# Attention inside an encoder layer: ScalarE's and GpSimd's side jobs dealt out one piece to a step

## The chip, the cores and the metric

The kernel runs on one core of a Trainium2 chip. Time is device time in microseconds (us) of one execution, from the profiler or from the runtime. The engines are TensorE (PE, its weight loads are shown as PEld), VectorE (DVE), ScalarE (ACT), GpSimd (POOL) and SyncE (SP, which only issues DMAs here). Each engine takes its instructions strictly one after the other, in an order fixed when the program is built; an instruction may carry waits for other engines or for DMAs, and everything behind it on its engine waits too.

## The reference

One encoder layer over 2048 tokens of width 1024, batch 1, float32:

```
h = rmsnorm(x, g1) * (1 + sc1) + sh1                   # shift, scale, gate from c
q, k, v of 8 stick-breaking heads and 8 chunk heads = h @ w_in      # head width 64
stick-breaking: z = q k^T / 8;  w = sigmoid(z) * prod of sigmoid(-z) over the later keys (strictly causal)
chunk heads:    rms-normed q, k;  softmax over own chunk of 64 + 8 earlier chunks, with a relative bias
x = x + gt1 * (concat(heads) @ w_o)
h = rmsnorm(x, g2) * (1 + sc2) + sh2
x = x + gt2 * (relu(h @ w1)^2 @ w2)
```

## The kernel before

Every float32 operand of a matmul is held as a high part and a remainder, both in a reduced float32 format, and each product is three matmuls. The program has four stretches: projections (to about 405 us), attention (405 to 1290 us), and then the rest of the output projection and the two large products of the MLP, to the end at 2572 us. The change touches attention alone.

Attention runs over units. A stick-breaking unit (`SB`, instructions `z`, `p`, `b`) is one head, a block g of 512 queries and a block c of 512 keys; a softmax unit (`CA`, instructions `cz`, `ct`, `s`, `e`) is one head and a block of 512 queries. Tokens are stored reversed, so a block's own keys come first: for g the units are c = g (the diagonal, where the four query rows of 128 see 512, 384, 256 and 128 keys), then c = g+1 to 3. The list is: for each head SB(2,2), SB(2,3), SB(3,3); all CA with g = 1 to 3; SB with g = 1 and g = 0; CA with g = 0. So the work turns three times from one kind to the other.

Each unit has four steps, one per 128 queries, and the main loop (from line 1298) issues one step after the other. In a step of a stick-breaking unit: TensorE turns a finished weight tile of eight steps earlier (`wt`, four transposes), ScalarE makes the sigmoid of the scores in place (`z`), VectorE scans it into running products (`p`), GpSimd subtracts neighbours (`b`, after a copy of one column into `p`), ScalarE and VectorE split the turned tile (`wth`, `wtl`), TensorE multiplies an older split tile into the accumulator (`acc`) and makes the scores of the next step (`z`). Scores and turned tiles take turns in one ring of four PSUM buffers (`z` of the pool `pz`), so a matmul into it needs VectorE to be done with the tile four back. In a softmax step VectorE adds bias and takes the maximum (`s`), ScalarE makes the exponential (`e`), and GpSimd scales it a step later. Between these TensorE works off pieces of other projections (`fill`, tiles `pf` and `po`), whose results ScalarE copies out (`stf`, `svf`).

When a unit is the last of its head and block, `finish` (line 788) runs a step later: ScalarE copies the two halves of the accumulator to `otmp` and `o`. After the second head of a pair, `total` has GpSimd add them (`o<-o,otmp`, 512 columns) in the next step, and `keep`, two steps later, has ScalarE make the high part (`os<-o`), GpSimd the remainder (`os<-o,os`), and SP store it. These jobs wait in the list `soon`: what a step puts there is issued in the next step, all of it, after that step's own work. At a turn they are put off three steps. `os` has one buffer, in pool `op`. In two blocks the output projection's rows are squared for the next norm (`square`, `add`, from line 1172) by the same list.

TensorE, VectorE, ScalarE and GpSimd keep the order in which the program issues instructions (class `Ordered`, line 34; its line 42 is therefore the line of nearly all rows of the profile). In attention SP's order is set by a scheduler.

Of the kernel before, what the change touches and what calls it, by code (L numbers as in the profile page):

```python
# [18 lines left out]
P = 128  # L19
S = 2048  # L20
D = 1024
HD = 64
# [3 lines left out]
TB = 512  # L26
# [53 lines left out]
def encoder_kernel(ctx, tc, xT, x3, wf, c, g1, g2, w_in, w_rest, gqk, bias, w_o, w1, w2, w_ada, b_ada, out):  # L80
    nc = tc.nc
    act, dve, pool, sp = nc.scalar, nc.vector, nc.gpsimd, nc.sync
# [7 lines left out]
    rows = {}  # L90
# [27 lines left out]
    zero = cpool.tile([P, 1], F32, name="zero")  # L118
# [9 lines left out]
    cols = cpool.tile([P, 184], F32, name="cols")  # L128
# [116 lines left out]
    if True:  # L245
# [200 lines left out]
        jobs = [(0, 3, 3), (0, 6, 3), (0, 6, 2), (2, 3, 2), (2, 2, 2), (0, 8, 3), (0, 8, 2), (2, 0, 2), (2, 1, 2)]  # L446
# [48 lines left out]
        whole = {}  # L495
# [7 lines left out]
        act, dve, pool = (Ordered(tc, e) for e in (act, dve, pool))  # L503
# [8 lines left out]
        first = (2, 0, 1)  # L512
# [37 lines left out]
        t = np_.tile([P, 4], F32, tag="nt", name="nta3")  # L550
# [199 lines left out]
    ph = ctx.enter_context(ExitStack())  # L750
    if True:
# [8 lines left out]
            out=held[:, :P], in_=held[:, :P], pattern=[[1, P]], base=0, channel_multiplier=-1,  # L760
# [27 lines left out]
        def finish(u):  # L788
            r = (u.h % 2) * HD
            q = HD - r  # L790
            if u.h % 2 == 0:
                pend["o", u.g] = [op.tile([P, TB], F32, tag=t, name=f"{t}{u.nm}", bufs=3) for t in ("o", "otmp")]
            o, tmp = pend["o", u.g]
            act.copy(tmp[r : r + HD, :], u.acc[q : q + HD, :])
            act.copy(o[r : r + HD, :], u.acc[r : r + HD, :])
            if u.h % 2:
                soon.append(lambda: total(u, o, tmp))

        def total(u, o, tmp):

            pool.tensor_tensor(o, o, tmp, op=ALU.add)
            soon.append(lambda: soon.append(lambda: keep(u, o)))

        def keep(u, o):

            os = op.tile([P, 2, TB], F32R, tag="os", name=f"os{u.nm}", bufs=1)
            split(os[:, 0, :], os[:, 1, :], o, pool)
            q = act if u is units[-1] else sp
            q.dma_start(scr_m[u.g, u.ca * 4 + u.h // 2], os.bitcast(F32))
            pairs[u.g] += 1  # L810
            if pairs[u.g] == KT and u.g > 0:
                filler.append(Filler(outproj, u.g))

        pend = {}
        pairs = [0] * NTB

        class Unit:
# [24 lines left out]

            def values(self, j):
                if j == 0 and self.first:
                    pend["acc"] = ppo.tile([P, TB], F32, tag="acc", name=f"acc{self.nm}")
                self.acc = pend["acc"]
                w = self.wt.pop(j)
                end = self.last and j == len(self.banks) - 1
                for m, (kb, q0, q1, at) in enumerate(self.banks[j]):
                    mine = slice(at * P, (at + q1 - q0) * P)  # L850
                    for l in range(2):
                        pe.matmul(
                            self.acc[:, q0 * P : q1 * P], self.v[kb // 4][:, kb % 4, :], w[l][:, mine],
                            start=self.first and j + m + l == 0, stop=end and l == 1 and m == len(self.banks[j]) - 1,
                        )
                if end:
                    soon.append(lambda: finish(self))

        DIAG = [[(3, 0, 4, 0)], [(2, 0, 3, 0), (0, 0, 1, 3)], [(1, 0, 2, 0)]]

# [302 lines left out]
        def finish_row(g, n, ps, xr):  # L1163

            residual(g, n, ps, xr)
            if g < 2 and drain:
                return
            stores.pop()()
            if g < 2:
                return  # L1170

            def square():
                sq = rows[g] if n == 0 else op.tile([P, TB], F32, tag="otmp", name=f"sq{g}_{n}", bufs=3)
                act.activation(sq, xr, AF.Square)
                if n:
                    soon.append(lambda: add(sq))

            def add(sq):
                pool.tensor_tensor(rows[g], rows[g], sq, op=ALU.add)
                if n == KT - 1:  # L1180
                    later.add(3, second)

            def second():
                pv = norm_sum(dense, rows[g], f"m{g}")

                def mean():
                    v = norm_mean(op, pv, f"m{g}")
                    y = op.tile([P, 4], F32, tag="ny", name=f"nym{g}")
                    rsqrt(y, v, op.tile([P, 4], F32, tag="nt", name=f"ntm{g}"))
                    later.add(3, lambda: spread(y))  # L1190

# [12 lines left out]
            if n == 0:  # L1204
                rows[g] = rp.tile([P, TB], F32, tag="r", name=f"r{g}")
            soon.append(square)

        LAG = 8
        STEPS = 4
# [12 lines left out]
        credit = 0.0  # L1222
        rest = 0
        late, soon, first, second = [], [], [], []

        def fill(part, more=0):

# [30 lines left out]
        def load(u):  # L1258
            nonlocal kp1
            if u.ca and u.g == 0 and u.h == 0:  # L1260
                narrow.close()
                kp1 = narrow.enter_context(tc.tile_pool(name="kp2", bufs=3, side="right"))
            need = (10, 11) if u.ca else (2, 3, 0, 1) + ((4, 5) if u.g == 0 else ())
            if u.g < 2:
                while not all((p, u.g) in have for p in need):
                    later.flush()
                    for job in soon:
                        job()
                    soon.clear()
                    while second:  # L1270
                        second.pop(0)()
                    force(filler[0])
            u.load()
# [17 lines left out]
        op = ph.enter_context(tc.tile_pool(name="op", bufs=2))  # L1291
        pado = ph.enter_context(tc.tile_pool(name="pado", bufs=1))
        pado.tile([P, 80], F32, tag="pad", name="pado")
        fp = ph.enter_context(tc.tile_pool(name="fp", bufs=3))
        wtp = ph.enter_context(tc.tile_pool(name="wtp", bufs=4))
        ldq = sp
        steps = [(u, st) for u in units for st in range(STEPS)]
        for i in range(len(steps) + LAG):
            if i % STEPS == 0:
                if i // STEPS + AHEAD < len(units):  # L1300
                    load(units[i // STEPS + AHEAD])
            vi = i - VST
# [12 lines left out]
            turned = front is not None and i and front.ca != steps[i - 1][0].ca  # L1315
            if front is not None and not turned:
                front.soft1(fs)
            while first:
                first.pop(0)()
            while second:  # L1320
                second.pop(0)()
            for j in js:
                back.parts(j)
                late.append((back, j))
            if turned:
                front.soft1(fs)
            if front is not None:
                front.soft2(fs)
            for job in done:
                if turned:  # L1330
                    later.add(3, job)
                else:
                    job()
            while len(late) > AVLAG:
                value(*late.pop(0))
            if i + 1 < len(steps):
                u, st = steps[i + 1]
                u.scores(st)
            fill(front.weight if front else 0.6, 6 if turned else 0)
            later.tick()  # L1340
        for u, j in late:
            value(u, j)
        while soon:
            soon.pop(0)()
        later.flush()
        while second:
            second.pop(0)()
# [15 lines left out]
    if True:  # L1363
# [34 lines left out]
        steps, jobs = [], {}  # L1398
# [475 lines left out]
```

## Time and profile before

| | |
|---|---|
| median of 3 runs | 2577.99 us (2572.71 to 2578.78; single runs 2578.78, 2577.99, 2572.71) |
| profiled execution, its own time | 2573.47 us |
| its span, first to last instruction | 2571.7 us |
| busy: PE, DVE, ACT, POOL | 2558.5, 1870.9, 1394.8, 904.3 us |
| TensorE clock granted | 1.0 throughout |
| attention, 421 to 1290 us: busy PE, DVE, ACT, POOL | 865.2, 727.8, 605.0, 566.2 of 869 us |

A row of the timeline reads: start, duration, engine, line, operation, what it writes <- what it reads (numbers of buffers left out), shape, how often in a row, and in brackets how long the engine had been idle and what ended it. A row of a group reads: engine, operation, names, shapes, count | busy us, mean ns of one | idle time before them and what ended most of it. A row by stage gives, for a stretch, its length and the busy us of PE, PEld, DVE, ACT and POOL with their counts, the granted clock, the DMA engines' share and GB/s.

### The profile page before, as it was taken

What the parts mean: (1) busy time and instruction counts of PE and PEld (TensorE: products, weight loads), DVE (VectorE), ACT (ScalarE), POOL (GpSimd) and SP (SyncE); (2) the same over time, 40 slices, a digit from 0 to 9 for tenths busy, and PEclk for the clock granted to TensorE, in tenths of its full rate; (3) what the DMA queues carried; (4) which work ended last, traced back from release to release, by engine and by line L of the source; (5) the groups of instructions that cost most, each with busy time, mean ns of one, the idle gap of its engine ahead of it and who ended that gap; (6) DMA issues with size and microseconds to landing.
All of it is one profiled execution on the core that took longest, in us unless ns stands there. A gap on an engine that the chain in (4) does not pass through costs nothing. (4 is left out here: it accounts for less than half of the span.)

```text
span 2571.7 us, 39222 instructions
## 1 busy us (share of the span) xinstructions
PE 2558.5 (99%) x12851; PEld 2153.6 (84%) x12851; DVE 1870.9 (73%) x3102; ACT 1394.8 (54%) x2596; POOL 904.3 (35%) x1232
## 2 busy tenths in 40 slices
PE   9999999999999999999999999999999999999999
PEld 7888888888889988888888888888888888888887
DVE  7656767887778999998687777768766565645655
ACT  7323434678886666666754444556444444544443
POOL 4330244766666666676513332100003323100000
PEclk9999999999999999999999999999999999999999
DMA  9879887789977686767787767866764344465574
GB/s 396 341 280 371 316 321 254 239 273 273 283 241 228 201 277 195 234 201 225 220 334 258 269 244 276 326 249 225 253 240 149 138 171 144 156 242 196 199 272 151
DMA packets 251263, 633.90 MB, mean 246 GB/s; under 512 B 28209, under 2 KB 56881, under 8 KB 241202
## 3 DMA queue, kind: packets, MB, share of 16 engines
q1 hardware_dynamic: 249760, 626.67, 70.7%
q10 hardware_dynamic: 1298, 4.72, 0.5%
q8 instruction: 101, 1.65, 0.3%
q14 instruction: 104, 0.85, 0.1%
HBM read 439.92 MB, written 191.37 MB: 245 GB/s over the span
## 5 line engine op out<-in xcount | busy, mean ns | idle before, releaser
L42 PE MATMUL ps<-oph,opv 128*128 128x512 f32 x2688 | 612.1, 389 | 0.2
L42 PE MATMUL ps<-h,opw 128*128 128x512 f32 x2664 | 604.2, 389 | 0.0
L42 PEld LDWEIGHTS ps<-oph,opv 128*128 128x128 f32 x2688 | 503.8, 188 | 106.5 <-DVE opv L42 1.2
L42 PEld LDWEIGHTS ps<-h,opw 128*128 128x128 f32 x2664 | 500.0, 188 | 103.9 <-DVE cx L42 0.2
L42 POOL TENSOR_TENSOR b<-p 128x512 f32<-128x512 f32 (+1 forms) x320 | 291.9, 912 | 201.8 <-DVE p L42 119.0
L42 ACT CAST wth<-wt 128x512 fp32r<-128x512 f32 (+1 forms) x432 | 244.1, 567 | 173.7 <-PE wt L42 169.5
L42 DVE TENSOR_TENSOR wtl<-wt,wth 128x512 fp32r<-128x512 f32 (+1 forms) x432 | 280.5, 653 | 63.9 <-ACT wth L42 62.9
L42 DVE TENSOR_TENSOR oph<-hw,oph 128x512 fp32r<-128x512 f32 x224 | 156.7, 699 | 211.4 <-ACT oph L42 211.4
L42 PE MATMUL pt<-w,ht 128*128 128x512 f32 x1248 | 288.0, 391 | 0.0
L42 ACT CAST oph<-hw 128x512 fp32r<-128x512 f32 x224 | 139.3, 622 | 273.5 <-PE ps L42 268.4
L42 POOL TENSOR_TENSOR ts<-w 128x512 f32<-128x512 f32 x32 | 47.2, 1474 | 661.8 <-DMA w<-in_w_dram 601.4
L42 PEld LDWEIGHTS pt<-w,ht 128*128 128x128 f32 x1248 | 233.0, 188 | 47.5
L42 DVE TENSOR_TENSOR_SCAN p<-z,p,zero 128x512 f32<-128x512 f32 x192 | 245.8, 1281 | 32.2 <-ACT z L42 21.3
L42 PE MATMUL acc<-wth,v 128*128 128x512 f32 (+3 forms) x544 | 217.3, 404 | 0.0
L42 ACT ACTIVATE z<-z 128x512 f32<-128x512 f32 (+1 forms) x320 | 165.9, 520 | 62.8 <-PE z L42 58.8
L42 PE MATMUL z<-k,q 128*128 128x512 f32 (+3 forms) x640 | 183.5, 368 | 2.4 <-DVE p L42 2.0
L42 PE MATMUL acc<-wtl,v 128*128 128x512 f32 (+3 forms) x544 | 181.2, 347 | 0.0
L42 DVE TENSOR_TENSOR opw<-w,opw 128x512 fp32r<-128x512 f32 x127 | 96.5, 762 | 113.2 <-ACT opw L42 113.1
L42 POOL TENSOR_TENSOR e<-e,cols 128x640 f32<-128x640 f32 (+1 forms) x128 | 143.0, 1121 | 93.5 <-DVE cols L42 71.9
L42 PE MATMUL wt<-ident,b 128*128 128x128 f32 x1088 | 166.0, 272 | 1.5 <-DVE wtl L42 0.7
L42 PE MATMUL po<-fx,ow 128*128 128x512 f32 x576 | 162.0, 393 | 0.0
L42 PEld LDWEIGHTS wt<-ident,b 128*128 128x128 f32 x1088 | 132.7, 140 | 28.7 <-DVE wtl L42 2.3
(200 smaller groups left out, 4088.9 us busy)
## 6 DMA issues: line engine op xcount, KB each, us to landing
hw<-scr_hid SPq DMA_DIRECT2D x112, 512.0 KB, 3.8
q<-scr_q SPq DMA_DIRECT2D x128, 256.0 KB, 4.7
w<-in_w_dram SPq DMA_DIRECT2D x64, 512.0 KB, 5.3
hw<-scr_s SPq DMA_DIRECT2D x64, 512.0 KB, 4.6
fw<-scr_w SPq DMA_DIRECT2D x28, 1024.0 KB, 7.2
k<-scr_k SPq DMA_DIRECT2D x224, 128.0 KB, 4.1
v<-scr_v SPq DMA_DIRECT2D x112, 256.0 KB, 4.0
wa<-in_w_ada_dram SPq DMA_DIRECT2D x48, 512.0 KB, 7.8
```

What stands on the lines that cost most here:

```text
L42: return lambda *x, **y: self.tc.keep_in_program_order(f(*x, **y))
```

## The change

The lists `acts` and `pools` take the side jobs of ScalarE and GpSimd. After a step's own work and the projections' copies, the loop issues one piece of `pools`, and then one of `acts` if there was no copy of a projection in this step (or more than three wait). At a turn and for two steps behind it neither is issued. `finish` puts in the copy to `otmp`, which puts the copy to `o` at the head of `acts`. Sums on GpSimd go in two halves of 256 columns (`halves`); the second half calls what follows. For a pair's sum that is `high`, appended to `acts`: the high part, whose tile now comes from the staging ring `st` of pool `fp` (four buffers instead of three). `keep` is then only the store. An accumulator is freed in time by the `while len(full) > 1` loops. At a turn a one-column activation of the coming kind is issued ahead of the splits.

```diff
         def finish(u):
             r = (u.h % 2) * HD
             q = HD - r
-            o, tmp = pend["o", u.g]
-            act.copy(tmp[r : r + HD, :], u.acc[q : q + HD, :])
-            act.copy(o[r : r + HD, :], u.acc[r : r + HD, :])
-            if u.h % 2:
-                soon.append(lambda: total(u, o, tmp))
-
-        def total(u, o, tmp):
-
-            pool.tensor_tensor(o, o, tmp, op=ALU.add)
-            soon.append(lambda: soon.append(lambda: keep(u, o)))
-
-        def keep(u, o):
-
-            os = op.tile([P, 2, TB], F32R, tag="os", name=f"os{u.nm}", bufs=1)
-            split(os[:, 0, :], os[:, 1, :], o, pool)
+            def first():
+                ...
+                act.copy(tmp[r : r + HD, :], u.acc[q : q + HD, :])
+                acts.insert(0, lambda: whole(o, tmp))
+
+            acts.append(first)
+            full.append(u)
+
+            def whole(o, tmp):
+                act.copy(o[r : r + HD, :], u.acc[r : r + HD, :])
+                full.pop()
+                if u.h % 2:
+                    halves(o, o, tmp, ALU.add, lambda: acts.append(lambda: high(u, o)))
+
+        def halves(out, a, b, op, end):
+
+            def half(n):
+                c = slice(n * TB // 2, (n + 1) * TB // 2)
+                pool.tensor_tensor(out[:, c], a[:, c], b[:, c], op=op)
+                if n:
+                    end()
+
+            for n in range(2):
+                pools.append(lambda n=n: half(n))
+
+        def high(u, o):
+            os = fp.tile([P, 2, TB], F32R, tag="st", name=f"os{u.nm}")
+            act.copy(os[:, 0, :], o)
+            halves(os[:, 1, :], o, os[:, 0, :].bitcast(F32), ALU.subtract, lambda: keep(u, os))
+
+        def keep(u, os):
             q = act if u is units[-1] else sp
...
                 act.activation(sq, xr, AF.Square)
                 if n:
-                    soon.append(lambda: add(sq))
+                    halves(rows[g], rows[g], sq, ALU.add, summed)
...
-            soon.append(square)
+            acts.append(square)
...
-        fp = ph.enter_context(tc.tile_pool(name="fp", bufs=3))
+        fp = ph.enter_context(tc.tile_pool(name="fp", bufs=4))
...
+            if turned:
+                act.activation(cols[:, 1:2], zero, AF.Exp if front.ca else AF.Sigmoid)
+            while len(full) > 1:
+                acts.pop(0)()
             for j in js:
                 back.parts(j)
...
+            hold = 3 if turned else max(0, hold - 1)
+            if not hold:
+                if pools:
+                    pools.pop(0)()
+                if acts and (not done or len(acts) > 3):
+                    acts.pop(0)()
             while len(late) > AVLAG:
```

How the order moves, at two places. In the names, `z_2_3_3_2` is the score tile of head 2, block 3, keys 3, step 2, and `os_1_2_3` belongs to heads 0 and 1 at block 2; the last number is a serial one. First the last two steps of a diagonal block, ScalarE and then GpSimd, before:

```order
L42 ACTIVATE z_2_3_3_3_4817<-z_2_3_3_3_4817 128x128
L42 CAST wth_2_2_2_2_4834<-wt_2_2_2_2_4825 128x256
L42 CAST os_1_2_3_4838<-o_0_2_3_4452 128x512
L42 ACTIVATE z_3_2_2_0_4844<-z_3_2_2_0_4844 128x512
L42 CAST wth_2_2_3_0_4867<-wt_2_2_3_0_4856 128x512
L42 COPY otmp_0_3_3_4557<-acc_1_3_3_4788 64x512
L42 COPY o_0_3_3_4556<-acc_1_3_3_4788 64x512
```

```order
L42 COPY p_2_3_3_2_4804<-ones 128x1
L42 TENSOR_TENSOR b_2_3_3_2_4803<-p_2_3_3_2_4804 128x256
L42 COPY p_2_3_3_3_4829<-ones 128x1
L42 TENSOR_TENSOR b_2_3_3_3_4828<-p_2_3_3_3_4829 128x128
L42 TENSOR_TENSOR os_1_2_3_4838<-o_0_2_3_4452,os_1_2_3_4838 128x512
```

and with the change:

```order
L42 ACTIVATE z_2_3_3_3_4817<-z_2_3_3_3_4817 128x128
L42 CAST wth_2_2_2_2_4834<-wt_2_2_2_2_4825 128x256
L42 CAST os_1_2_3_4839<-o_0_2_3_4452 128x512
L42 ACTIVATE z_3_2_2_0_4843<-z_3_2_2_0_4843 128x512
L42 CAST wth_2_2_3_0_4866<-wt_2_2_3_0_4855 128x512
L42 COPY otmp_0_3_3_4557<-acc_1_3_3_4787 64x512
```

```order
L42 COPY p_2_3_3_2_4803<-ones 128x1
L42 TENSOR_TENSOR b_2_3_3_2_4802<-p_2_3_3_2_4803 128x256
L42 TENSOR_TENSOR o_0_2_3_4452<-o_0_2_3_4452,otmp_0_2_3_4453 128x256
L42 COPY p_2_3_3_3_4829<-ones 128x1
L42 TENSOR_TENSOR b_2_3_3_3_4828<-p_2_3_3_3_4829 128x128
L42 TENSOR_TENSOR o_0_2_3_4452<-o_0_2_3_4452,otmp_0_2_3_4453 128x256
```

ScalarE's copy `os` has kept its place. The sum `o` that it reads stood behind `b_2_3_3_1`, ahead of the first row shown of GpSimd; now its halves stand behind `b_2_3_3_2` and `b_2_3_3_3`, the second in the copy's own step. ScalarE's copies `otmp` and `o` no longer follow each other. The second place is a step of 512 columns, the sum of heads 6 and 7 of the softmax group, GpSimd before and after:

```order
L42 TENSOR_TENSOR b_0_1_3_2_9520<-p_0_1_3_2_9521 128x512
L42 COPY p_0_1_3_3_9547<-p_0_1_2_3_9443 128x1
L42 TENSOR_TENSOR b_0_1_3_3_9546<-p_0_1_3_3_9547 128x512
L42 TENSOR_TENSOR os_7_2_9556<-o_6_2_9134,os_7_2_9556 128x512
L42 COPY p_1_1_1_0_9580<-ones 128x1
```

```order
L42 TENSOR_TENSOR b_0_1_3_2_9557<-p_0_1_3_2_9558 128x512
L42 TENSOR_TENSOR o_6_2_9169<-o_6_2_9169,otmp_6_2_9170 128x256
L42 COPY p_0_1_3_3_9585<-p_0_1_2_3_9478 128x1
L42 TENSOR_TENSOR b_0_1_3_3_9584<-p_0_1_3_3_9585 128x512
L42 TENSOR_TENSOR o_6_2_9169<-o_6_2_9169,otmp_6_2_9170 128x256
```

Here too the halves stand behind the last two `b`, and ScalarE's copy is in the same step, with the change:

```order
L42 ACTIVATE z_0_1_3_3_9572<-z_0_1_3_3_9572 128x512
L42 CAST wth_0_1_1_2_9590<-wt_0_1_1_2_9581 128x256
L42 CAST os_7_2_9595<-o_6_2_9169 128x512
L42 ACTIVATE z_1_1_1_0_9599<-z_1_1_1_0_9599 128x512
L42 CAST wth_0_1_2_0_9622<-wt_0_1_2_0_9611 128x512
```

More of the change, by code (lines that the diff above doesn't have):

```diff
@@ L790, in finish @@
             q = HD - r
-            if u.h % 2 == 0:
-                pend["o", u.g] = [op.tile([P, TB], F32, tag=t, name=f"{t}{u.nm}", bufs=3) for t in ("o", "otmp")]
-            o, tmp = pend["o", u.g]
-            act.copy(tmp[r : r + HD, :], u.acc[q : q + HD, :])
-            act.copy(o[r : r + HD, :], u.acc[r : r + HD, :])
-            if u.h % 2:
-                soon.append(lambda: total(u, o, tmp))
-        def total(u, o, tmp):
-            pool.tensor_tensor(o, o, tmp, op=ALU.add)
-            soon.append(lambda: soon.append(lambda: keep(u, o)))
-        def keep(u, o):
-            os = op.tile([P, 2, TB], F32R, tag="os", name=f"os{u.nm}", bufs=1)
-            split(os[:, 0, :], os[:, 1, :], o, pool)
+            def first():
+                if u.h % 2 == 0:
+                    pend["o", u.g] = [op.tile([P, TB], F32, tag=t, name=f"{t}{u.nm}", bufs=3) for t in ("o", "otmp")]
+                o, tmp = pend["o", u.g]
+                act.copy(tmp[r : r + HD, :], u.acc[q : q + HD, :])
[20 more added lines that the diff above has]
+        def keep(u, os):
             q = act if u is units[-1] else sp
@@ L856, in values @@
                 if end:
-                    soon.append(lambda: finish(self))
+                    finish(self)
         DIAG = [[(3, 0, 4, 0)], [(2, 0, 3, 0), (0, 0, 1, 3)], [(1, 0, 2, 0)]]
@@ L1175, in square, with summed @@
                 if n:
-                    soon.append(lambda: add(sq))
-            def add(sq):
-                pool.tensor_tensor(rows[g], rows[g], sq, op=ALU.add)
+                    halves(rows[g], rows[g], sq, ALU.add, summed)
+            def summed():
                 if n == KT - 1:
@@ L1224, in encoder_kernel @@
         late, soon, first, second = [], [], [], []
+        acts, pools, full = [], [], []
+        hold = 0
         def fill(part, more=0):
@@ L1266, in load @@
                     later.flush()
+                    while pools:
+                        pools.pop(0)()
                     for job in soon:
@@ L1321, in encoder_kernel @@
                 second.pop(0)()
+            if turned:
+                act.activation(cols[:, 1:2], zero, AF.Exp if front.ca else AF.Sigmoid)
+            while len(full) > 1:
+                acts.pop(0)()
             for j in js:
@@ L1333, in encoder_kernel @@
                     job()
+            hold = 3 if turned else max(0, hold - 1)
+            if not hold:
+                if pools:
+                    pools.pop(0)()
+                if acts and (not done or len(acts) > 3):
+                    acts.pop(0)()
             while len(late) > AVLAG:
@@ L1342, in encoder_kernel @@
             value(u, j)
-        while soon:
-            soon.pop(0)()
+        while soon or acts or pools:
+            for jobs in (soon, acts, pools):
+                while jobs:
+                    jobs.pop(0)()
         later.flush()
```

## The prediction

> **What bounds the kernel now.** I read the page's busy shares first, then the busy times by stage, then who waited for whom in the attention stage (400 to 1290 us), then the rows around single waits.
>
> ```profile
> PE 2558.5 (99%) x12851; PEld 2153.6 (84%) x12851; DVE 1870.9 (73%) x3102; ACT 1394.8 (54%) x2596; POOL 904.3 (35%) x1232
> ...
> L42 PE MATMUL ps<-h,opw 128*128 128x512 f32 x2664 | 604.2, 389 | 0.0
> ```
>
> TensorE is busy for 99% of the span. The second row gives its pace: 2664 matmuls of 512 columns in 604.2 us are one per 0.227 us, while each is drawn 0.389 us long. So a drawn gap on TensorE is 0.16 us shorter than what was really lost. The change moves no matmul that matters (same count, and but for eight tiny sums and spreads of a norm the same order), so the time can only move by what TensorE waits in attention. The next rows are TensorE's weight loads by what they waited for in that stage: total us, times, longest.
>
> ```profile
> PEld z L42 <- DVE p L42: 6.5, 14, 1.1
> PEld wt L42 <- DVE wtl L42: 3.8, 11, 1.0
> PEld wt L42 <- DVE p L42: 1.0, 1, 1.0
> ```
>
> About 11.3 us in 26 waits, part of it behind running matmuls: that is the ceiling of any gain here, 0.4% of the time. What is waited for is a PSUM tile of the ring "z" (four buffers, shared by scores and transposes): VectorE must have read the old tile (the scan p, or wtl), and the scan needs ScalarE's sigmoid. So the path that can hurt is ScalarE, then VectorE, then TensorE. VectorE has little room to catch up in the stick-breaking stage (third busy time of the row, after PE and PEld: 293.30 of 321.00 us, 91%):
>
> ```profile
> 860.00:1181.00 321.00, 320.21 (x1828) 271.39 (x1827) 293.30 (x352) 204.92 (x377) 217.91 (x372) 1.00 0.69 224
> ```
>
> **The change, part by part.** These groups of the stage carry the prices (count | busy us, mean ns | idle before, releasers):
>
> ```profile
> L42 ACT COPY o<-acc 64x512 f32<-64x512 f32 x64 | 37.2, 581 | 0.8
> L42 ACT CAST os<-o 128x512 fp32r<-128x512 f32 x32 | 19.8, 618 | 8.2 <-POOL o L42 5.9 <-DMA scr_m<-os 2.1
> L42 POOL TENSOR_TENSOR o<-o,otmp 128x512 f32<-128x512 f32 x32 | 41.3, 1290 | 8.3 <-ACT o L42 8.3
> L42 POOL TENSOR_TENSOR b<-p 128x512 f32<-128x512 f32 x224 | 233.1, 1040 | 171.4 <-DVE p L42 105.6 <-PE z L42 28.7 <-PE wt L42 24.0
> L42 POOL TENSOR_TENSOR b<-p 128x256 f32<-128x256 f32 x32 | 19.6, 614 | 6.9 <-PE wt L42 3.4 <-DVE p L42 1.9
> L42 POOL TENSOR_TENSOR b<-p 128x128 f32<-128x128 f32 x32 | 12.8, 399 | 5.1 <-DVE p L42 3.2 <-PE z L42 0.3
> ```
>
> *Halves.* A sum o or os of 1.29 us becomes two of 256 columns. Between 0.65 us (half of 1.29) and 0.76 us (b's ratio 614/1040 times 1.29); I take 0.74, nearer to b, whose widths show a fixed part. Some 0.2 us more per sum on GpSimd, which is 35% busy: nothing by itself, and if that cover is gone the 78 added halves are at most 8 us of GpSimd, not of the path.
>
> *The place of the sum is what counts.* Before, the whole sum o was queued two steps ahead of ScalarE's copy os<-o. Now the first half follows GpSimd's b one step ahead, the second half follows the b of **the same step** as the copy, and the copy goes out at once behind it (the job that issues the second half puts the copy into ScalarE's empty list, which is read next). ScalarE takes its instructions in order, so it stands at the copy until sigmoid, scan, b and half of that step have run through three engines; behind it are queued the next sigmoid and the next wth, for which VectorE and then TensorE wait. By the order of the two engines, of 32 sums 16 fall in stick-breaking steps, and in 11 of them copy and second half share a step: 5 in the last step of a diagonal block (b of 128 columns) and 6 in a step of 512 columns. In the other 5 another job pushed the copy a step or more on.
>
> What such a stand costs TensorE, two rows of before tell:
>
> ```profile
> 468.92 0.62 ACT L42 CAST os<-o 128x512 fp32r<-128x512 f32 x1 [2.10 <-DMA scr_m<-os]
> ...
> 471.96 0.66 PE L42 MATMUL wt<-ident,b 128*128 128x128 f32 x4 [0.56 <-DVE p L42]
> ...
> 473.73 0.50 PE L42 MATMUL z<-k,q 128*128 128x512 f32 x1 [0.65 <-DVE p L42]
> ...
> 1033.79 0.62 ACT L42 CAST os<-o 128x512 fp32r<-128x512 f32 x1 [1.36 <-POOL o L42]
> ...
> 1036.28 0.50 PE L42 MATMUL z<-k,q 128*128 128x256 f32 x2 [0.30 <-DVE p L42]
> ```
>
> ScalarE stood 2.10 us and TensorE lost 0.56+0.65, with 0.16 us hidden in each 1.53 us; it stood 1.36 us and TensorE lost 0.30+0.16 = 0.46 us. So 0.6 to 0.9 us of a stand is free, the rest is paid. Now the new stands. Diagonal block, the sum of heads 0 and 1 at block 2:
>
> ```profile
> 458.52 0.68 DVE L42 TENSOR_TENSOR_SCAN p<-z,held 128x256 f32<-128x256 f32 x1
> ...
> 459.70 0.41 DVE L42 TENSOR_TENSOR_SCAN p<-z,held 128x128 f32<-128x128 f32 x1
> ...
> 459.96 0.37 ACT L42 CAST wth<-wt 128x256 fp32r<-128x256 f32 x1 [0.65 <-PE wt L42]
> ...
> 460.83 0.57 ACT L42 ACTIVATE z<-z 128x512 f32<-128x512 f32 x1
> ...
> 461.51 1.23 DVE L42 TENSOR_TENSOR_SCAN p<-z,held 128x512 f32<-128x512 f32 x1 [0.72 <-ACT z L42]
> ...
> 463.56 0.45 PE L42 MATMUL z<-k,q 128*128 128x256 f32 x2
> ```
>
> The scan of 256 ends at 459.20; b 0.61, half 0.74, the small copy p with its gap 0.2, b of 128 0.40, half 0.74: 461.95. ScalarE is at the copy at 460.33, so it stands 1.6 us. The copy takes 0.6, the sigmoid starts at 462.55 and not 460.83, the scan ends 1.72 us late, 464.46 for 462.74. TensorE wanted that buffer at 463.56, 0.82 us after its release: **0.9 us lost**, five times: 4.5 us.
>
> Steps of 512 columns, the costliest and the cheapest of the six:
>
> ```profile
> 784.96 1.28 DVE L42 TENSOR_TENSOR_SCAN p<-z,p,zero 128x512 f32<-128x512 f32 x1
> ...
> 786.41 0.37 ACT L42 CAST wth<-wt 128x256 fp32r<-128x256 f32 x1 [0.41 <-PE wt L42]
> ...
> 786.73 1.28 DVE L42 TENSOR_TENSOR_SCAN p<-z,p,zero 128x512 f32<-128x512 f32 x1
> ...
> 787.48 0.58 ACT L42 ACTIVATE z<-z 128x512 f32<-128x512 f32 x1
> ...
> 788.24 1.22 DVE L42 TENSOR_TENSOR_SCAN p<-z,held 128x512 f32<-128x512 f32 x1
> ...
> 789.79 0.45 PE L42 MATMUL z<-k,q 128*128 128x256 f32 x2
> ...
> 928.66 0.59 ACT L42 CAST wth<-wt 128x512 fp32r<-128x512 f32 x1
> ...
> 928.72 1.28 DVE L42 TENSOR_TENSOR_SCAN p<-z,p,zero 128x512 f32<-128x512 f32 x1 [0.52 <-ACT z L42]
> ...
> 929.59 0.58 ACT L42 ACTIVATE z<-z 128x512 f32<-128x512 f32 x1 [0.34 <-PE z L42]
> ...
> 930.50 1.27 DVE L42 TENSOR_TENSOR_SCAN p<-z,p,zero 128x512 f32<-128x512 f32 x1
> ...
> 933.05 0.63 PE L42 MATMUL z<-k,q 128*128 128x512 f32 x2
> ```
>
> First: scan end 786.24, b to 787.34, half to 788.08, copy p, b to 789.31, half to 790.05; ScalarE stands from 786.78, 3.3 us. Its sigmoid starts at 790.65 for 787.48, the scan, 0.65 us later, at 791.3 for 788.24; slack 789.79 - 789.46 = 0.33; lost 2.7 us. Second: scan end 930.00, b to 931.10, half to 931.84, ScalarE stands 2.6 us from 929.25; the sigmoid is 2.85 us late, the scan 2.6 us; slack 933.05 - 931.77 = 1.28; lost 1.3 us. Middle **2.0 us**, six times: 12 us. Together +16.5 us. Bounds: halves of 0.65 us and 0.9 us free in each, +11; only 0.33 us free in each, +22.
>
> In softmax steps the scores' tile is freed by VectorE without ScalarE, so only wth is held up; I take 0, at most 16 times 0.2 = 3 us.
>
> *What goes.* The stand of 2.10 us for a store (the copy's one-buffer home becomes one of four): 1.5 us. The two copies of 0.58 us that stood in one step and now stand in two, the sums of 1.29 us on GpSimd that made os<-o wait (5.9 us in the group, 0.46 of it paid at 1036): perhaps 3.5 us of the rest of the ceiling. And the tables, at the first turn to softmax:
>
> ```profile
> 563.25 0.59 ACT L42 CAST wth<-wt 128x512 fp32r<-128x512 f32 x1 [2.14 <-PE wt L42]
> ...
> 565.63 1.28 ACT L42 ACT_TABLE_LOAD   x1 [1.80 <-DVE cols L42]
> 566.93 0.83 ACT L42 ACTIVATE e<-s,cols 128x640 f32<-128x640 f32 x1
> ...
> 569.10 0.73 PE L42 MATMUL cz<-k,q 128*128 128x512 f32 x2 [0.47 <-DVE wtl L42]
> ```
>
> The load of 1.28 us moves into the idle 2.14 us ahead of 563.25, the exponential starts up to 1.28 us sooner and the 0.47+0.16 us at 569.10 go; the other two turns show no such gap. [...]
>
> Gains 1.5 + 3.5 + 0.6, say 6 us (at least 2.5, at most 9). The store moves later in SP's queue with its copy; nothing waits for it but the output projection much later, so 0. The accumulator is freed one step later, since its second copy waits a step; it has two buffers and the next head's takes the other, so 0, and without that cover one copy of 0.58 us a head. **Sum: +16.5 - 6 = +10.5 us** (from +2 to +19.5).
>
> **Rivals.** (1) *No difference.* The free part of a stand is larger than two rows tell and the losses come to some 6 us, as much as the gains: 2573 to 2580 us. For it: os<-o waited 5.9 us before and TensorE paid little of it. Against: those waits were short, the new ones are 1.6 to 3.3 us. (2) *Faster.* GpSimd has the halves done in time after all, since it no longer runs 1.29 us at a stretch, and only the gains are left: 2573.5 - 6 = 2567, at the ceiling 2564. It decides if the wait before os<-o stays under 0.9 us. Against it stands the order itself. (3) *Slower still.* VectorE, 91% busy, cannot make up what it loses, and the stands are paid whole: 5 x 1.6 + 6 x 2.9 = 25.5, less 2.5: 2596. It decides if TensorE's wait follows ScalarE's one to one. (4) *The shared ring.* The copy now takes turns with the projections' staging tiles; if four copies stood for stores as the one at 468.92 did, 4 x 1.5 = 6 us on top: 2590 us.
>
> **How the numbers follow.** The profiled execution took 2573.47 us (span 2571.7); + 10.5 is 2584. The median of the three runs is 2577.99, two of them near 2578.5 and one, like the profiled one, near 2573; on the median it would be 2588.5. I say 2586. This kernel's runs tell 0.3% (7.7 us) from no change. Chances: forecast 0.55, of which an eighth lies within 0.3%; rival 1 0.28; rival 3 0.08; rival 4 0.04; rival 2 0.05. So slower 0.48 + 0.12 = 0.60, same 0.07 + 0.28 = 0.35, faster 0.05. Range 2575 (rival 1 in its upper half) to 2597 (rival 3, or the forecast's +19.5 on the median).
>
> **What would show it.** In the groups, os<-o must wait for POOL o some 25 us in all where it was 5.9; TensorE's weight loads must wait over 20 us for DVE p; the store wait of 2.1 us must be gone and the three table loads stand ahead of a wth. Busy times of TensorE stay, its stage from 421 to 1290 us grows. If os<-o waits under 10 us, the order was read wrongly; if it waits 25 us and the weight loads still 11, the free part was.

## The result, and the profile after

| | before | with the change |
|---|---|---|
| median of 6 runs each, us | 2577.39 (2572.71 to 2579.00) | 2592.92 (2590.46 to 2594.92) |
| profiled execution, span, us | 2571.7 | 2591.7 |
| ratio of the runs | | 1.0064, 95% interval 1.0052 to 1.0075 |

The kernel became slower by 0.64%, about 16.5 us (13 to 19 by the interval). The two profiled executions lie 20.0 us apart, because the one of the kernel before took 2573.47 us, some 4 us under that kernel's median. The forecast was 10.5 us more and 2586 us, with a range of 2575 to 2597. The projections and the MLP take their old time; the whole growth is in attention. Over the same 893 us, from 406 to 1299 us, TensorE was busy as follows, first before, then with the change (a row by stage: length, busy us and count of PE, PEld, DVE, ACT, POOL, clock, DMA share, GB/s):

```profile
406.00:1299.00 893.00, 888.62 (x5399) 772.68 (x5398) 745.27 (x1393) 617.91 (x1224) 576.87 (x855) 1.00 0.77 240
```

```profile
406.00:1299.00 893.00, 875.53 (x5321) 760.62 (x5320) 741.47 (x1384) 611.16 (x1220) 587.12 (x933) 1.00 0.75 233
```

Thirteen us of matmul time are missing. The groups of the changed kernel that answer to those of the prediction (count | busy us, mean ns | idle before, releasers):

```profile
L42 ACT CAST os<-o 128x512 fp32r<-128x512 f32 x32 | 19.8, 618 | 37.2 <-POOL o L42 35.6 <-DMA k<-scr_k 1.5
L42 POOL TENSOR_TENSOR o<-o,otmp 128x256 f32<-128x256 f32 x64 | 47.0, 736 | 7.4 <-ACT o L42 7.4
L42 ACT ACT_TABLE_LOAD x3 | 3.8, 1283 | 0.0
```

ScalarE now stands 35.6 us in front of the copy `os<-o`, waiting for GpSimd's sum, where it stood 5.9 us; the halves take 0.736 us (0.74 was assumed); the wait of 2.1 us for a store is gone; the table loads follow without idle time. The 1.5 us that the first row puts down to a DMA are a stand too: that copy starts at 852.29 us, in the moment in which the sum's second half ends. TensorE's weight loads (total us, times, longest):

```profile
PEld z L42 <- DVE p L42: 19.7, 21, 2.8
...
PEld pf L42 <- DMA fw<-scr_w: 2.0, 1, 2.0
PEld acc L42 <- ACT o L42: 1.6, 2, 0.9
```

The first row was 6.5 us in 14 waits. The last two rows have no counterpart before. Three stands, each with the row of TensorE that pays for it (in the brackets the idle time and what ended it):

```profile
461.83 0.62 ACT L42 CAST os<-o 128x512 fp32r<-128x512 f32 x1 [1.59 <-POOL o L42]
...
464.31 0.50 PE L42 MATMUL z<-k,q 128*128 128x256 f32 x2 [0.69 <-DVE p L42]
...
793.58 0.62 ACT L42 CAST os<-o 128x512 fp32r<-128x512 f32 x1 [3.47 <-POOL o L42]
...
794.79 1.23 DVE L42 TENSOR_TENSOR_SCAN p<-z,held 128x512 f32<-128x512 f32 x1 [3.00 <-ACT z L42]
...
796.07 0.50 PE L42 MATMUL z<-k,q 128*128 128x256 f32 x2 [2.66 <-DVE p L42]
...
1051.74 0.62 ACT L42 CAST os<-o 128x512 fp32r<-128x512 f32 x1 [2.81 <-POOL o L42]
...
1054.21 0.44 PE L42 MATMUL z<-k,q 128*128 128x128 f32 x2 [2.17 <-DVE p L42]
```

This is the chain of the prediction, link by link: copy, then the sigmoid behind it (the scan's bracket names it, `<-ACT z`), then the scan, then the matmul that needs the buffer. With the 0.16 us that a drawn gap hides (matmuls drawn 0.389 us long, one per 0.227 us, in the prediction's rows), these three cost TensorE 0.85, 2.8 and 2.3 us.

For the comparison below, "lost" is counted from the starts of TensorE's matmuls in attention: the time from one start to the next, less the median of the same pair of matmuls (the first by its shape, the second by names and shape), wherever the excess is over 0.2 us. Before it is 7.4 us, with the change 22.1 us.

### The profile page after: what moved, and what is told of

Same layout as the page of the kernel before. It is cut to its first block, busy times and chain, and to the rows that moved or that the text cites. A ratio compares the mean times of both kernels' runs of the same rounds, so it can differ in the third digit from the quotient of the medians.

```text
span 2591.7 us, 39288 instructions
## 1 busy us (share of the span) xinstructions
PE 2565.1 (99%) x12851; PEld 2155.4 (83%) x12851; DVE 1876.5 (72%) x3102; ACT 1392.8 (54%) x2599; POOL 914.6 (35%) x1310
## 4 chain that ended last, share of the span: by engine, by line
PE 89%; DVE 3%; ACT 2%; POOL 2%; DMA 2%; issue 1%; SPq 0%; DVEq 0%; POOLq 0%; ACTq 0%
PE ps L42 46%; PE pt L42 11%; PE acc L42 6%; PE wt L42 6%; PE pf L42 5%; PE z L42 4%; PE po L42 4%; PE pq L42 3%; PE cz L42 2%; DVE p L42 1%; POOL b L42 1%; PE ct L42 1%; PE px L42 1%; POOL o L42 1%; ACT z L42 0%
```

## The experiments

Theory: ScalarE stands at the copy, because the copy is issued in the step of the sum's second half. Rivals: the halves themselves, the copy's new home in the shared ring, the second copy of the accumulator a step later, or the store's place in SP's queue carry the loss.

### The copy one step later, and two steps later

```diff
-halves(o, o, tmp, ALU.add, lambda: acts.append(lambda: high(u, o)))
+halves(o, o, tmp, ALU.add, lambda: later.add(1, lambda: acts.append(lambda: high(u, o))))
```

(and the loop that empties the lists at the end empties this one too; the second kernel has `later.add(2, ...)`.)

> The change, with the copy os<-o put into ScalarE's list one step after the sum's second half instead of at once; halves, home, tables and the later copies otmp and o are the change's. My theory (ScalarE stands at the copy): the step is some 3 us long, so stands of 1 to 3 us go; os<-o waits under 8 us for POOL o in attention (35.6 with the change, 5.9 before), TensorE's weight loads wait under 12 us for DVE p (19.7, and 6.5 before), and the time falls below the kernel before by the gains forecast: about 2572 to 2577 us, ratio 0.998 to 1.000. Rival (the sums in halves, the shared ring, or the later copies of the accumulator carry the loss): os<-o no longer waits, but the time stays at 2588 to 2594 us, ratio 1.004 to 1.007.

> As copy_1_later, but two steps later. My theory: no stand at os<-o at all (under 3 us in all), 2571 to 2577 us, ratio 0.9975 to 1.000, within 2 us of copy_1_later. What the other parts of the change cost then stands alone: with the late second copy of the accumulator TensorE's acc may still wait 1 to 3 us for ACT o. Rival (the cost lies in the other parts): 2588 to 2594 us. A third way (the copy one or two steps on meets another late step, or pushes the later pieces of ScalarE's list on): between, 2580 to 2587 us.

One step later: 2572.19 us, ratio to before 0.9985 (0.9976 to 0.9994). Two steps later: 2572.51 us, 0.9988 (0.9979 to 0.9997). The group of the copy, then the weight loads, in attention, one step later:

```profile
L42 ACT CAST os<-o 128x512 fp32r<-128x512 f32 x32 | 19.7, 616 | 7.3 <-POOL o L42 6.9 <-DMA k<-scr_k 0.4
```

```profile
PEld z L42 <- DVE p L42: 3.8, 8, 1.1
PEld po L42 <- issue: 1.7, 1, 1.7
PEld acc L42 <- ACT o L42: 1.5, 2, 0.7
```

This one step of distance takes 0.79% (20.4 us of 2577) off the changed kernel. Halves, shared ring, late second copy and early tables are all still there, so none of them carries the loss. The wait of `acc` for ScalarE's late second copy stands as before the edit, 1.5 us; counted in starts it is 1.5 us where the same two places lost 0.5 in the kernel before, so its price is 1.0 us. The row `po` is one wait that ends at 1290.5 us, for which this view shows no releaser. More room than one step brings nothing that these runs can tell.

### The sum beside its copy, in the kernel before

```diff
-soon.append(lambda: total(u, o, tmp))                      # in finish
+soon.append(lambda: soon.append(lambda: soon.append(lambda: total(u, o, tmp))))
-    soon.append(lambda: soon.append(lambda: keep(u, o)))   # in total
+    keep(u, o)
```

> The kernel before, with one thing moved: the sum o (512 columns, whole) is issued in the step of its copy os<-o, right ahead of it, instead of two steps earlier. One-buffer home, list of jobs, tables, copies of the accumulator as before. My theory: this alone makes ScalarE stand; 16 of the 32 copies lie in stick-breaking steps, those behind a 128-column b lose about 0.9 + 0.5 us each, those behind a 512-column b about 2 + 0.5: with 10 and 6 of them, 14 + 15 = 29 us at most, 15 us if a third of it is free or made up; 2590 to 2606 us, ratio 1.005 to 1.011, and os<-o waits 30 to 55 us for POOL o. Rival (other parts of the change carry the loss): 2576 to 2580 us, ratio 0.999 to 1.001.

2610.90 us, ratio 1.0139 (1.0126 to 1.0153): the place of the sum alone makes the kernel before slower, and by more than the change does. The upper figure of the expectation, 29 us, was too low: 36 us were lost (0.0139 of 2577).

```profile
L42 ACT CAST os<-o 128x512 fp32r<-128x512 f32 x31 | 19.2, 620 | 60.6 <-POOL o L42 60.6
```

```profile
462.19 0.62 ACT L42 CAST os<-o 128x512 fp32r<-128x512 f32 x1 [1.65 <-POOL o L42]
...
464.68 0.50 PE L42 MATMUL z<-k,q 128*128 128x256 f32 x2 [0.75 <-DVE p L42]
...
644.40 1.09 PE L42 MATMUL wt<-ident,e 128*128 128x128 f32 x8 [0.98 <-DVE wtl L42]
...
804.27 0.62 ACT L42 CAST os<-o 128x512 fp32r<-128x512 f32 x1 [3.75 <-POOL o L42]
...
806.75 0.80 PE L42 MATMUL z<-k,q 128*128 128x256 f32 x2 [3.04 <-DVE p L42]
```

Two things were missing from it. Some softmax steps pay too: ahead of the row at 644.40 ScalarE had stood 1.92 us at a copy, had hardly been idle since, and its splits came late. Not every such stand is paid. And TensorE's granted clock was halved for five stretches of 3.41 us, which the last section takes up.

### Whole sums

```diff
-            for n in range(2):
-                pools.append(lambda n=n: half(n))
+            def one():
+                pool.tensor_tensor(out, a, b, op=op)
+                end()
+
+            pools.append(one)
```

First in the change as it is, then together with the copy one step later:

> The change, with each sum on GpSimd as one instruction of 512 columns (1.29 us by the kernel before) issued where the first half was; the copy still goes out in the step of the sum, behind it. My theory: the copy is one step earlier, but it still stands behind the b of its own step and a whole sum, 1.04 + 1.29 us behind the scan's end against 1.04 + 0.74; so os<-o waits 25 to 50 us in all for POOL o and the time is 2586 to 2597 us, ratio 1.003 to 1.008, no better than the change. Rival (halves, their fixed part or their number, carry the loss): 2575 to 2580 us.

> As copy_1_later, with each sum on GpSimd whole (one instruction of 512 columns, 1.29 us) instead of in halves. What the halves are worth by themselves, the copy's place aside: theory, nothing that can be measured, since GpSimd has slack: 2571 to 2574 us, ratio 0.998 to 0.9995, at most 10 us of waits of os<-o. Rival (a whole sum holds up the next b, as halves are meant to avoid): 2576 us or more.

Whole sums in the change: 2605.03 us, ratio 1.0122 (1.0106 to 1.0137), 15 us slower than with halves by the ratios (12 by the medians) and 8 us above the upper end that was expected. The waiting copy group rose to 48.2 us:

```profile
L42 ACT CAST os<-o 128x512 fp32r<-128x512 f32 x32 | 19.8, 618 | 51.5 <-POOL o L42 48.2 <-DMA q<-scr_q 3.3
```

```profile
797.99 1.28 POOL L42 TENSOR_TENSOR o<-o,otmp 128x512 f32<-128x512 f32 x1
799.30 0.62 ACT L42 CAST os<-o 128x512 fp32r<-128x512 f32 x1 [4.26 <-POOL o L42]
...
801.84 0.46 PEld L42 LDWEIGHTS z<-k,q 128*128 128x128 f32 x2 [3.05 <-DVE p L42]
```

Whole sums with the copy one step later: 2577.09 us, ratio 1.0004 (0.9995 to 1.0013). Against 0.9985 for the same with halves the halves are worth about 5 us here, which was not expected. Where they lie:

```profile
L42 ACT CAST os<-o 128x512 fp32r<-128x512 f32 x32 | 19.7, 616 | 13.4 <-POOL o L42 12.7 <-DMA q<-scr_q 0.6
```

```profile
PEld z L42 <- DVE p L42: 6.5, 11, 1.4
```

The copy still waits 12.7 us for the sum where it waits 6.9 with halves, and TensorE's loads 6.5 for 3.8: a whole sum of 1.29 us behind the `b` of its step is not always done one step on. So this is the same mechanism with less of it, and it holds some 2.6 of the 5 us (lost, as defined above: 8.8 us against 6.2). The rest is not traced to a cause.

### One kind of pair at a time

The copy one step later for the pairs of softmax heads alone, then for those of stick-breaking heads alone:

```diff
-halves(o, o, tmp, ALU.add, lambda: acts.append(lambda: high(u, o)))
+halves(o, o, tmp, ALU.add, lambda: later.add(1, ...) if u.ca else acts.append(...))
```

> The change, with the copy os one step later for the pairs of softmax heads alone (three of their copies, behind the second turn, share a step with their sum in the change). By the change's trace TensorE lost 0.9 + 2.8 + 1.0 = 4.7 us behind these three, and two stretches of half clock (2 x 1.7 us) and a wait of 2.0 us for a load fw stand in the same 30 us. If these hang on the three stands: 4.7 + 5.4 = 10 us less than the change, about 2583 us, ratio to before 1.002 to 1.003. If the clock and the load are something else: 4.7 less, 2588 us, 1.0045. By my prediction's equal price of 2.0 us a full step, three of them: 6 less, 2587.

> The change, with the copy os one step later for the pairs of stick-breaking heads alone. By the change's trace TensorE lost 0.85 + 0.46 + 0.91 (diagonal blocks of g = 2), 0.50 + 0.37 + 1.45 + 2.34 + 1.76 (g = 1 and 0) and 0.2 + 0.7 in steps behind: 9.5 us; so about 2583 us, ratio 1.002 to 1.003. If the two losses add up, what this run and late_softmax_pairs gain on the change sums to the 20.7 us by which copy_1_later is faster than it. If the loss lies behind the second turn alone, this stays at 2590 or more.

Softmax pairs late: 2584.61 us, ratio 1.0036 (1.0023 to 1.0049), 0.28% or 7.2 us less than the change. Stick-breaking pairs late: 2580.68 us, 1.0023 (1.0013 to 1.0032), 0.41% or 10.6 us less. Together 17.8 of the 20.4 us: they add up within the intervals. For the copy and for TensorE, softmax pairs late:

```profile
L42 ACT CAST os<-o 128x512 fp32r<-128x512 f32 x32 | 19.8, 617 | 24.0 <-POOL o L42 23.9
```

```profile
PEld z L42 <- DVE p L42: 15.0, 17, 2.3
PEld pf L42 <- DMA fw<-scr_w: 1.7, 1, 1.7
```

and stick-breaking pairs late:

```profile
L42 ACT CAST os<-o 128x512 fp32r<-128x512 f32 x32 | 19.8, 618 | 21.1 <-POOL o L42 21.1
```

```profile
PEld z L42 <- DVE p L42: 7.9, 10, 2.8
PEld pf L42 <- DMA fw<-scr_w: 2.1, 1, 2.1
```

The three softmax copies behind the second turn were thus worth 7.2 us, between the 4.7 of their stands alone and the 10 with all that stood around them. What did not go with them is the wait for `fw`: it is there with softmax pairs late too, so it does not hang on those stands, as one branch of the expectation had it. The two stretches of half clock did go with them; in that run one other stands at 1046.68 us.

### The home and the tables alone

```diff
-            os = op.tile([P, 2, TB], F32R, tag="os", name=f"os{u.nm}", bufs=1)
+            os = fp.tile([P, 2, TB], F32R, tag="st", name=f"os{u.nm}")
...
-        fp = ph.enter_context(tc.tile_pool(name="fp", bufs=3))
+        fp = ph.enter_context(tc.tile_pool(name="fp", bufs=4))
...
+            if turned:
+                act.activation(cols[:, 1:2], zero, AF.Exp if front.ca else AF.Sigmoid)
```

in the kernel before, everything else as it was:

> The kernel before, with two parts of the change alone: os gets its home from the ring st of four buffers, and a one-column activation at each turn loads the tables early. The jobs and sums stay as before. My prediction: the stand of 2.1 us for a store goes (1.5 us on TensorE) and the gap behind the first turn (0.6 us): some 2 us less, ratio 0.999 to 1.000; the remaining 2.5 us that copy_1_later is faster than before then lie in the dealt-out copies and sums. Rival: all of the 4.5 us lies here, 2572 us, and the dealing out is worth nothing. Second rival (shared ring): copies stand for stores in the ring, 2580 us or more.

2572.72 us, ratio 0.9990 (0.9981 to 0.9999), 2.6 us less.

```profile
L42 ACT CAST os<-o 128x512 fp32r<-128x512 f32 x32 | 19.8, 619 | 6.6 <-POOL o L42 6.2 <-DMA fw<-scr_w 0.2
L42 ACT ACT_TABLE_LOAD x3 | 3.8, 1283 | 0.0
```

No copy waits for a store any more, so the shared ring costs the copies nothing, and the tables' idle 3.6 us is gone. These two edits are a small gain by themselves, barely clear of the noise. Whether the dealing out of copies and sums adds to it (0.9985 with it, 0.9990 without) these runs can't tell: the intervals overlap.

### The store out of SP's queue

```diff
-            q = act if u is units[-1] else sp
+            q = act if u is units[-1] else pool
```

> The change, with the stores scr_m<-os issued by GpSimd instead of SP (the copy stands as in the change). Theory of SP's queue: in the change the store waits on SP for GpSimd up to 5.1 us and holds the loads k and fw behind it; TensorE then waited 2.0 us for fw at 818 us and ran 3.4 us at half clock. With the store out of that queue both go: 2.0 to 3.7 us less, 2589 to 2591 us, and the waits of L825 are gone from SP. Rival: the load is late for another reason, or the issue on GpSimd costs as much: 2592 to 2595 us.

2596.75 us, ratio 1.0079 (1.0063 to 1.0094): not faster, and if anything slower. TensorE no longer waits for `fw` at all, but GpSimd now issues the store in its own order, and waits first:

```profile
POOL scr_m L42 <- POOL os L42: 11.2, 28, 0.4
POOL scr_m L42 <- DVE wtl L42: 3.8, 3, 3.0
```

```profile
L42 ACT CAST os<-o 128x512 fp32r<-128x512 f32 x32 | 19.8, 619 | 40.6 <-POOL o L42 40.5
```

These 15 us make the sums still later, and the copy stands 40.5 us instead of 35.6. So the run shows what lateness on GpSimd costs; it doesn't settle what the store in SP's queue cost.

### Both copies of the accumulator in one step for softmax heads

On top of the copy one step later:

```diff
-                acts.insert(0, lambda: whole(o, tmp))
+                if u.ca:
+                    whole(o, tmp)
+                else:
+                    acts.insert(0, lambda: whole(o, tmp))
```

> As copy_1_later, and for softmax heads both copies of the accumulator are issued in one step again, as in the kernel before. In copy_1_later TensorE's acc waited twice for ACT o, 1.5 us in all (softmax stage). Theory: both waits are gone and nothing stands in their place, 1.0 to 1.5 us less than copy_1_later, about 2571 us, ratio to before 0.998. Rival: two copies of 0.58 us in one softmax step delay the exponentials by as much, 2572 to 2573, ratio 0.9985.

2573.74 us, ratio 0.9994 (0.9985 to 1.0003): no gain. One of the two `acc` waits went, but the places of the sums and copies shifted too, and one stand of the change came back (2.2 us on ScalarE at 786.40 us, 1.6 us lost on TensorE at 788.89), as did a late load `fw`. TensorE's loads by what they waited for:

```profile
PEld z L42 <- DVE p L42: 5.3, 9, 1.6
...
PEld pf L42 <- DMA fw<-scr_w: 1.5, 1, 1.5
```

### The runs side by side

Lost as defined above; half clock is the time for which the granted clock read 0.5 in attention. Half of it is counted as lost, an estimate from two rows of the change: ten matmuls `pf` of 256 columns were drawn 1.36 us long together at a clock of 1.00 (from 815.70 us), five 1.27 us at 0.50 (from 822.63 us). All of the profiled executions, us:

| kernel | lost | half clock | lost + half of it, against before | span against before |
|---|---|---|---|---|
| before | 7.4 | 0 | 0 | 0 |
| the change | 22.1 | 6.8 | +18.2 | +20.0 |
| copy one step later | 6.2 | 0 | -1.2 | -2.6 |
| copy two steps later | 6.1 | 0 | -1.3 | -1.0 |
| softmax pairs late | 17.4 | 3.4 | +11.7 | +13.5 |
| stick-breaking pairs late | 11.7 | 3.4 | +6.0 | +5.0 |
| whole sums | 31.1 | 3.4 | +25.5 | +27.3 |
| sum beside copy | 36.3 | 17.1 | +37.5 | +39.4 |
| store by GpSimd | 25.6 | 13.7 | +25.1 | +24.2 |
| home and tables alone | 6.3 | 0 | -1.1 | -1.0 |
| whole sums, copy one step later | 8.8 | 0 | +1.4 | +3.4 |
| both copies in one step | 7.8 | 0 | +0.4 | +2.8 |

TensorE's waits and its clock explain every span to within 2.4 us. In the row of the sum beside its copy some 1.8 us are counted twice (matmuls that start late only because the clock is halved), in that of the store by GpSimd 1.0 us; without them the first misses its span by some 4 us.

## Why the prediction was right, and where it was not

**The cause was right.** That ScalarE would stand at the copy because it shares a step with the sum's second half, read from the order of the instructions, is what the runs show: moving only the copy takes the loss away, moving only the sum in the kernel before brings it. The copy waited 35.6 us (some 25 forecast), TensorE's loads 19.7 us for the scan, just short of the "over 20" named as the sign. Of the 35.6 and the 1.5 put down to a DMA, the eleven stands of the forecast make 23.5 us (25.5 worked out); 4.2 are two copies that another job had pushed on, and 9.4 lie in eight softmax steps, which the forecast priced at nothing on TensorE and where it lost 0.3. One sign did not come: TensorE's busy time was to stay and rose from 2558.5 to 2565.1 us. The half clock, at which five matmuls `pf` of 256 columns were drawn 0.415 us long each (from 822.63 us) and ten at full clock 0.282 us (from 815.70 us), makes about half of this by estimate (6.8 us at 0.5); the rest was not followed up.

**The stands: +16.5 forecast, 13.4 measured.** The five behind a `b` of 128 columns lost 0.85, 0.46, 0.91, 0.50 and 0.37 us, together 3.1 (forecast 5 x 0.9 = 4.5). The six behind 512 columns lost 0.90, 2.83, 1.00, 1.45, 2.34 and 1.76 us, together 10.3 (forecast 6 x 2.0 = 12). The one worked out as the costliest, 2.7 us, lost 2.83, and ScalarE stood there 3.47 us for the 3.3 worked out. What was free of a stand lay between 0.5 and 1.4 us, wider than the 0.6 to 0.9 read from two rows. Taking the middle of the dearest and the cheapest of six erred by 0.3 us a step, since the step taken for the cheapest (1.3 worked out, 1.45 lost) was not: two others lost 0.90 and 1.00. The lower bound of +11 for all stands does not come out of its own terms: with halves of 0.65 us and 0.9 us free in each they give about 13.7, and the measured 13.4 lies just under that, because up to 1.4 us were free.

**The copies that another job had pushed on: 0 forecast, 0.9 us.** Two of those five still stood, at 470.75 and 551.85 us, and cost 0.2 and 0.7 us.

**The accumulator freed a step later: 0 forecast, 1.2 us.** The second buffer was not cover enough in the softmax stage: the rows `acc <- ACT o` above, 1.6 us in two waits, count 1.64 us in starts where the same places lost 0.47 before. The prediction had named the price without that cover, 0.58 us a head, but it fell at two heads alone.

**The store in SP's queue: 0 forecast; a load came 2.0 us late.** SP's rows ahead of it, and TensorE's:

```profile
SPq L825 <- POOL p L42: 14.3, 3, 5.1
```

```profile
812.16 0.33 SPq L825 DMA_DIRECT2D scr_m<-os  x1
812.89 0.45 SPq L778 DMA_DIRECT2D k<-scr_k  x1
813.46 0.52 SPq L1089 DMA_DIRECT2D fw<-scr_w  x1
...
818.03 0.40 PE L42 MATMUL pf<-fw,fx 128*128 128x256 f32 x2
...
820.26 0.74 PE L42 MATMUL pf<-fw,fx 128*128 128x256 f32 x4 [1.83 <-DMA fw<-scr_w]
```

Between 760 and 830 us the store (L825) waited on SP for GpSimd up to 5.1 us, and the loads behind it went out only then. "Nothing waits for it" overlooked what stands behind it in the same queue. But that the store alone makes `fw` late is argued, not shown: with the copy one step later the store still waited up to 4.5 us there and `fw` cost 0.4, and taking it to GpSimd changed too much at once.

**The gains: 6 forecast, 2.7 seen in the change.** The store wait at 468.92 (1.5 us) and the gap at the first turn (0.6 us) went as said; the other 0.6 us is what many places of 0.2 to 0.8 us leave, some gone and some new. At that turn:

```profile
562.70 1.28 ACT L42 ACT_TABLE_LOAD   x1
564.00 0.20 ACT L42 ACTIVATE cols<-zero 128x1 f32<-128x1 f32 x1
564.81 0.59 ACT L42 CAST wth<-wt 128x512 fp32r<-128x512 f32 x1 [0.61 <-PE wt L42]
...
567.16 0.83 ACT L42 ACTIVATE e<-s,cols 128x640 f32<-128x640 f32 x1 [1.76 <-DVE cols L42]
```

The exponential starts 2.35 us after the split, where it was 3.68 us. It waits for VectorE, not for a table. The load now has no wait around it: the instruction ahead ends 0.02 us before it, and the next starts 0.02 us behind it. The further 3.5 us for dealing out copies and sums were an estimate; the runs leave 1.3 us of it net (0.9990 against 0.9985), which their intervals do not tell from nothing.

**The clock: not in the sum at all, 3.4 us.** No step reckoned with it; see below.

Put together: 13.4 + 0.9 + 1.2 + 2.0 + 3.4 - 2.7 = 18.2. The last term is what the balance of the lost time leaves, so this is the table's figure again; what it is to be held against is the 20.0 us between the profiled spans. The forecast's 16.5 - 6 = 10.5 missed 7.5 us of side effects and put the gains 3.3 us too high, and it put the stands 3.1 us too high. That the last error made up for part of the first two was luck; even so the forecast lies 6 us under the measured 16.5.

**The rivals.** No difference: refuted, the free part is not that large. Faster: the wait had to stay under 0.9 us in each stand, and no stand was that short (its lowest time, 2564 us, goes by gains of 9 us; the ceiling of 11.3 us would give 2562). Paid whole: the eleven stands lasted 23.5 us and 13.4 were paid, so no. Shared ring: refuted by the home and the tables alone.

## What to carry to other kernels

When a producer is cut into pieces that are dealt out one to a step, its consumer should not be issued in the step of the last piece on an engine that works in order: here one step of distance was enough, and it was worth 20 us of 2577. Read who shares a step from the order of instructions on the two engines; price a stand by the slack of the buffer that is waited for at that place, not by one figure for all. And look down each queue at what stands behind a transfer that waits: "nothing needs it" says nothing of the ones behind.

## What the runs showed of the hardware

In the change TensorE's granted clock read 0.50 for 3.41 us twice in attention: behind a wait drawn 2.66 us long that ends at 796.07 us, and behind one of 1.83 us that ends at 820.26 us. Rows by stage of the changed kernel (PE busy is the first busy time, the clock stands third from the end):

```profile
794.12:797.53 3.41, 1.46 (x12) 1.46 (x13) 2.74 (x4) 3.36 (x8) 1.34 (x2) 1.00 0.89 217
797.53:800.94 3.41, 3.41 (x17) 3.40 (x16) 2.71 (x5) 1.51 (x5) 3.17 (x8) 0.50 0.16 63
...
818.01:821.42 3.41, 1.58 (x12) 1.35 (x11) 2.60 (x4) 0.58 (x1) 1.93 (x4) 1.00 1.02 347
821.42:824.84 3.42, 3.42 (x15) 3.22 (x14) 1.65 (x2) 1.64 (x3) 0.79 (x3) 0.50 1.07 364
...
1050.12:1053.53 3.41, 1.92 (x12) 1.30 (x10) 0.38 (x2) 1.78 (x5) 1.72 (x3) 1.00 0.84 278
1053.53:1056.94 3.41, 2.73 (x17) 2.33 (x18) 3.35 (x6) 1.73 (x5) 2.53 (x5) 1.00 0.08 26
```

The two drops begin 23.89 us apart, 7 times 3.413 us, and each lasts 3.41 us. In the 3.41 us ahead of them TensorE stood idle in one piece for 1.95 and 1.83 us (length less busy time), 57 and 54% of the stretch. From the two drops attention is laid off here in windows of this length. The wait of 2.17 us that ends at 1054.21 us falls across the edge of two of them, with 1.49 us in the first, and no drop follows. No other window at full clock in attention was idle for more than 1.51 us in the change (from 1176.41 us) or 1.21 us in the kernel before (from 470.93 us, the windows laid off from a drop at its end), and no drop followed any of these. In the sum beside its copy drops begin at 805.86 and 1000.42 us, 57 times 3.413 us apart; the 3.42 us ahead of them were idle for 2.15 and 2.08 us. The first of the two lasted two windows, to 812.68 us, though the window from 805.86 us was idle for only 0.89 us. So by these rows the same wait costs itself alone or an estimated 1.7 us more (half of 3.41), by where it falls. The eleven executions of the copy one step later, in whose trace no wait in attention but one that ends at 1290.5 us costs more than 0.8 us, show a mean clock of 1.000 each; the six of the change 0.998 to 0.999. Of 23 executions of the kernel before beside the last two experiments, 16 at a mean of 1.000 took 2574.3 us in the median and 7 below it 2578.2, so part of what that kernel's runs scatter goes with the clock. This is observed, not tested by an experiment of its own.
